# The opening of a two-layer encoder: the conditioning vector spread by its transfer, the vector table fetched first, low halves of the first weights on VectorE

## The chip, the cores and the metric

The kernel runs on one core of a Trainium2 chip. The metric is the device time of one execution in microseconds (us). Before the change it is 1388.13 us, the median of 3 runs (1387.73 to 1389.67). TensorE (PE) multiplies matrices, and its weight loads are shown as PEld; VectorE (DVE) and GpSimd (POOL) work elementwise on two tensors, ScalarE (ACT) on one; SyncE (SP) issues all the transfers of this kernel, in one queue.

## What is computed

The reference is an encoder of two layers over 512 tokens of width 1024. Each layer has a token mixer (layer 0 a gated short convolution, layer 1 a recurrent one) and an MLP. Each of these four parts is preceded by an RMS norm whose result is scaled and shifted by vectors that come from a conditioning vector `c`:

```
c_act = silu(c)
mod = c_act @ ada_w[i] + ada_b[i]          # six vectors of 1024 in each layer
sh1, sc1, gt1, sh2, sc2, gt2 = split(mod)
h = rmsnorm(x) * norm_g * (1 + sc1) + sh1
bch = h @ conv_w_in                        # layer 0: 1024 -> 3 x 1024
```

The change lies in these first lines of layer 0: `c_act`, the first two of its six vectors, the first norm, and the first part of `h @ conv_w_in`.

## The kernel before

Activations are kept transposed: 8 blocks of 128 features on the partitions by 512 tokens. To keep float32 accuracy every operand of a product is split in a high half (a rounded copy, made on ScalarE) and a low half (the original less the high one, a two-tensor subtraction), and a product is three passes: high by high, low by high, high by low.

The opening goes like this. SP issues `c` (one row of 1024 on one partition, L100), eight blocks of `x` (L102), the table `vec` of all small vectors (L103), and then for each of 8 blocks k two tiles of adaptation weights (`ada0`, 512 KB each, L374) and one tile of the first projection (`cin_a`, 128 x 896, L379). A transfer further down the queue waits until the eighth before it has landed, or until the buffer it fills is free.

ScalarE takes the sigmoid of `c`, VectorE multiplies it with `c` (L388), TensorE multiplies the row by a column of ones (L392) so that it stands on all 128 partitions, and ScalarE copies it from PSUM to `cb` (L397) between two squares. Meanwhile ScalarE squares the blocks of `x` (L226, L230) and VectorE adds them up (L231). TensorE sums over partitions (L402); square root (L406), reciprocal (L407) and four small products (L412, L413) spread the norm's factor. `keep_warm` matmuls (L365), whose result nobody reads, stand between.

Then comes a loop over the 8 blocks; I call it the block loop. For each k VectorE takes a dot of `cb` with an adaptation tile for the shift (L205, the first dot), makes the scale g0 (L420), the normed block t (L255), takes the dot for the scale of block k+1 (L205, the second dot), and makes the low half of h (L257). ScalarE makes the high half of h (L256) and the high half of the weights (L131), GpSimd their low half (L132). TensorE does 21 matmuls per block (L433: seven output tiles, three passes). After the loop the other 17 output tiles follow, one `linear` each of 24 matmuls (L171 to L173), on weights `wmain` (L136) whose low halves VectorE makes (L132).

TensorE, VectorE and ScalarE run the block loop in the order in which the code is written (the manual schedule). A scheduler orders what follows, and it may draw later instructions in between.

Of the kernel before, what the change touches and what calls it, by code (L numbers as in the profile page):

```python
# [10 lines left out]
F32 = mybir.dt.float32  # L11
F32R = mybir.dt.float32r
AF = mybir.ActivationFunctionType
ALU = mybir.AluOpType
# [3 lines left out]
P = 128  # L18
D = 1024
T = 512  # L20
# [34 lines left out]
def trunk(ctx: ExitStack, tc: tile.TileContext, x_in, vec_in, c_in, ada0, ada, cin_a, wmain,  # L55
          l1_in, g1_in, l2_in, g2_in, out, stop=None):
    nc = tc.nc
    V, A, G, PE = nc.vector, nc.scalar, nc.gpsimd, nc.tensor
# [9 lines left out]
    def uid():  # L68
        cnt[0] += 1
        return cnt[0]  # L70

    def bank(shape=(P, T)):
        return ps.tile(list(shape), F32, tag="ps", name=f"ps{uid()}")

    def sm(shape, bufs=2):
        return const.tile(list(shape), F32, tag="s" + "_".join(map(str, shape)), name=f"sm{uid()}", bufs=bufs)

    def big(shape=(P, 2, T), dt=F32R):
        return pool.tile(list(shape), dt, tag="b", name=f"b{uid()}", bufs=NBIG)
# [4 lines left out]
    def tmp(dt=F32):  # L84
        return pool.tile([P, T], dt, tag="t", name=f"t{uid()}", bufs=NTMP)

    def pair():
        t = big()
        return t[:, 0], t[:, 1]
# [6 lines left out]
    vec = const.tile([P, NVEC * KB], F32, name="vec")  # L96
    cb = big((P, D), F32)
    junk = big((P, D), F32)
    cr, cs = (big((P, D), F32)[0:1] for _ in range(2))
    nc.sync.dma_start(cr, c_in)  # L100
    for k in range(KB):
        nc.sync.dma_start(x[k], x_in[:, k * T:(k + 1) * T])  # L102
    nc.sync.dma_start(vec, vec_in)  # L103

    def vv(n, k=None):
        o = VEC[n] * KB
        return vec[:, o:o + KB] if k is None else vec[:, o + k:o + k + 1]
# [3 lines left out]
    ones = const.tile([P, P], F32, name="ones")  # L111
# [9 lines left out]
    def behind(ins, other):  # L121

        tc.add_manual_dep(ins.ins, other.ins.name, mybir.DependencyInfo(mybir.DependencyClass.NoSync,
                                                                        mybir.DependencyReason.DATA), reason="slots")
# [5 lines left out]
    def split(dst_hi, dst_lo, src, eng=None):  # L130
        A.copy(dst_hi, src)  # L131
        return (eng or V).tensor_tensor(dst_lo, src, dst_hi.bitcast(F32), op=ALU.subtract)  # L132
# [71 lines left out]
    def ada_dot(l, v, m, w):  # L204
        return V.tensor_tensor_reduce(junk, w, cb, 1.0, vv(f"ab{l}{v}", m), ALU.mult, ALU.add, mods[l, v][:, m:m + 1])  # L205
# [15 lines left out]
        ada_pump(max(0, want - ast["n"]))  # L221


    def add_sq(acc, k, sl):
        if k == 0:
            A.activation(acc[:, sl], x[k][:, sl], AF.Square)  # L226
        else:
            w = sl.stop - sl.start
            t = tmp()
            A.activation(t[:, :w], x[k][:, sl], AF.Square)  # L230
            V.tensor_tensor(acc[:, sl], acc[:, sl], t[:, :w], op=ALU.add)  # L231

    def new_acc():
        return tmp()
# [17 lines left out]
    def h_block(k, sl, pb, g, sh, hi, lo=None):  # L252
        w = sl.stop - sl.start
        t = tmp()
        V.scalar_tensor_tensor(t[:, :w], x[k][:, sl], g[:, k:k + 1], pb, op0=ALU.mult, op1=ALU.mult)  # L255
        A.activation(hi[:, sl], t[:, :w], AF.Identity, bias=sh[:, k:k + 1])  # L256
        return lambda: V.scalar_tensor_tensor(lo[:, sl], t[:, :w], sh[:, k:k + 1], hi[:, sl].bitcast(F32),  # L257
                                              op0=ALU.add, op1=ALU.subtract)
# [45 lines left out]
    def out_linear(acts, gt, nxt, side=lambda: None):  # L304

        n = NLAST
        for m in range(KB - n):
            pt = linear(1, acts)[0]
            residual(pt, m, FULL, gt)
            add_sq(nxt.acc, m, FULL)  # L310
            side()
        ws = w_take(n)

        def mm(pt, i, sl):
            for k in range(KB):
                passes(pt[:, sl], ws[i][0][:, k, :], ws[i][1][:, k, :], acts[k][0][:, sl], acts[k][1][:, sl],
                       k == 0, k == KB - 1)

        last_tiles(mm, gt, nxt)

    def last_tiles(mm, gt, nxt, spare=NFIRST):
        n = NLAST
        pt = [bank() for _ in range(n)]
        for sl in HALVES:
            for i in range(n):
                mm(pt[i], i, sl)
                if sl.start == 0 and i < spare:
                    w_conv(wst["pos"] + i + 1, True)
                residual(pt[i], KB - n + i, sl, gt)
                add_sq(nxt.acc, KB - n + i, sl)  # L330
                if sl.start:
                    for k in range(KB * i // n, KB * (i + 1) // n):
                        nxt.block(k, HALVES[0])
            if sl.start == 0:
                w_ahead()
                nxt.chain(sl)
# [26 lines left out]
    def keep_warm(n, after=None):  # L363
        for _ in range(n):
            m = PE.matmul(warm, ones, cmask, start=True, stop=True)  # L365
            if after is not None:
                behind(m, after)
# [3 lines left out]
    def ada_load(k):  # L371
        arw[k] = [big((P, D), F32) for _ in range(2)]
        for i in (1, 0):
            first = nc.sync.dma_start(arw[k][i], ada0[k, i])  # L374
        return first

    def weights(k):
        wr = big((P, NPRE * P), F32)
        nc.sync.dma_start(wr, cin_a[k])  # L379
        w = big((P, NPRE * P)), big((P, NPRE * P))  # L380
        split(*w, wr, G)
        return w

    g0 = const.tile([P, KB], F32, name="gs00")
    ada_load(0)
    with tc.manual_schedule(engines={mybir.EngineType.PE, mybir.EngineType.DVE, mybir.EngineType.Activation}):
        A.activation(cs, cr, AF.Sigmoid)
        V.tensor_tensor(cs, cr, cs, op=ALU.mult)  # L388
        keep_warm(NWARM)
        pcs = [bank() for _ in range(2)]  # L390
        for i in range(2):
            PE.matmul(pcs[i], ones[0:1], cs[:, i * T:(i + 1) * T], start=True, stop=True)  # L392
        acc = new_acc()
        for k in range(KB):
            add_sq(acc, k, FULL)
            if k in (5, 6):
                A.copy(cb[:, (k - 5) * T:(k - 4) * T], pcs[k - 5])  # L397
        keep_warm(2)
        A.activation(sm((P, 1)), epsn, AF.Sqrt)
        pm = bank((P, 4))  # L400
        for b in range(4):
            PE.matmul(pm[:, b:b + 1], acc[:, b * P:(b + 1) * P], ones[:, 0:1], start=True, stop=True)  # L402
        ada_dot(0, 1, 0, arw[0][1])
        keep_warm(1)
        sd = sm((P, 4))
        A.activation(sd, pm, AF.Sqrt, scale=1.0 / D, bias=epsn)  # L406
        V.reciprocal(sd, sd)  # L407
        pb = bank()
        dg = tmp()
        for b in range(4):  # L410
            c = slice(b * P, (b + 1) * P)
            V.tensor_scalar(dg[:, c], ident, sd[:, b:b + 1], None, op0=ALU.mult)  # L412
            PE.matmul(pb[:, c], ones, dg[:, c], start=True, stop=True)  # L413
        keep_warm(1)
        w = weights(0)
        h = []
        pts = [bank() for _ in range(NPRE)]
        for k in range(KB):
            ada_dot(0, 0, k, arw[k][0])
            V.scalar_tensor_tensor(g0[:, k:k + 1], mods[0, 1][:, k:k + 1], 1.0, vv("ng00", k), op0=ALU.add,  # L420
                                   op1=ALU.mult)
            h.append(pair())
            lo = h_block(k, FULL, pb, g0, mods[0, 0], *h[k])
            whi, wlo = w
            if k + 1 < KB:
                first = ada_load(k + 1)
                ada_dot(0, 1, k + 1, arw[k + 1][1])
            lo()
            if k + 1 < KB:
                w = weights(k + 1)  # L430
            for a, b in ((whi, 0), (wlo, 0), (whi, 1)):
                for i in range(NPRE):
                    PE.matmul(pts[i], a[:, i * P:(i + 1) * P], h[k][b], start=k == 0 and a is whi and not b,  # L433
                              stop=k == KB - 1 and b == 1)
# [5 lines left out]
    for j in range(KB):  # L440
        pc, pv, pg = [pts[3 * j + i] if 3 * j + i < NPRE else linear(1, h)[0] for i in range(3)]
        cs = tmp()
# [3 lines left out]
        t = tmp()  # L446
# [198 lines left out]
    with tc.manual_schedule(engines=MANUAL):  # L645
# [258 lines left out]
        t = 30  # L904
# [455 lines left out]
```

## Time and profile before

| | us |
|---|---|
| median of the runs | 1388.13 |
| the profiled execution | 1386.2 |
| its span, first to last instruction | 1384.2 |
| TensorE busy | 1309.3 (95%) |
| VectorE busy | 850.8 (61%) |
| ScalarE busy | 544.2 (39%) |
| GpSimd busy | 216.3 (16%) |

The mean granted clock of TensorE is 0.973 of full speed. TensorE carries 82% of the chain of work that ended last, VectorE 11%. In the first of 40 slices of the span (34.6 us each) TensorE is busy six tenths, in the second eight, and nine from the third on nearly everywhere.

### The profile page before, as it was taken

What the parts mean: (1) busy time and instruction counts of PE and PEld (TensorE: products, weight loads), DVE (VectorE), ACT (ScalarE), POOL (GpSimd) and SP (SyncE); (2) the same over time, 40 slices, a digit from 0 to 9 for tenths busy, and PEclk for the clock granted to TensorE, in tenths of its full rate; (3) what the DMA queues carried; (4) which work ended last, traced back from release to release, by engine and by line L of the source; (5) the groups of instructions that cost most, each with busy time, mean ns of one, the idle gap of its engine ahead of it and who ended that gap; (6) DMA issues with size and microseconds to landing.
All of it is one profiled execution on the core that took longest, in us unless ns stands there. A gap on an engine that the chain in (4) does not pass through costs nothing.

```text
span 1384.2 us, 20374 instructions
## 1 busy us (share of the span) xinstructions
PE 1309.3 (95%) x8182; PEld 1069.6 (77%) x8182; DVE 850.8 (61%) x1264; ACT 544.2 (39%) x924; POOL 216.3 (16%) x249
## 2 busy tenths in 40 slices
PE   6899999999999999899897599999989999999997
PEld 3688889888888888787576477777788888888886
DVE  6996668746747565736869835566574344343445
ACT  4233334323233234447552357765344133232331
POOL 2300020000000003523428512232300000000000
PEclk8999999999999999999999799999999999999998
DMA  8466432735646355301283413322222232222221
GB/s 326 148 241 244 184 122 107 262 127 202 231 147 250 136 197 190 119 16 61 73 236 110 107 52 124 102 84 67 72 77 76 91 107 92 94 104 91 98 101 61
DMA packets 83440, 184.44 MB, mean 133 GB/s; under 512 B 35377, under 2 KB 37681, under 8 KB 83346
## 3 DMA queue, kind: packets, MB, share of 16 engines
q1 hardware_dynamic: 83346, 183.14, 38.3%
q8 instruction: 64, 1.05, 0.3%
q14 instruction: 30, 0.25, 0.1%
HBM read 168.44 MB, written 13.63 MB: 132 GB/s over the span
## 4 chain that ended last, share of the span: by engine, by line
PE 82%; DVE 11%; ACT 3%; issue 2%; DMA 1%; POOL 1%; SPq 0%; DVEq 0%; ACTq 0%; POOLq 0%
PE ps L171 24%; PE ps L172 23%; PE ps L173 23%; DVE b L205 2%; DVE t L231 1%; DVE b L852 1%; DVE b L848 1%; PE ps L1002 1%; PE ps L1080 1%; PE ps L1047 1%; PE ps L1116 1%; PE ps L1099 1%; DVE w L132 1%; ACT w L131 1%; PE ps L630 1%
## 5 line engine op out<-in xcount | busy, mean ns | idle before, releaser
L173 PE MATMUL ps<-b,w 128*128 128x512 f32 (+1 forms) x1486 | 565.1, 380 | 10.5 <-DVE w L132 9.2
L171 PE MATMUL ps<-b,w 128*128 128x512 f32 (+1 forms) x1486 | 573.1, 386 | 1.1 <-DVE b L302 1.0
L172 PE MATMUL ps<-b,w 128*128 128x512 f32 (+1 forms) x1486 | 566.1, 381 | 5.1 <-POOL b L132 5.0
L131 ACT CAST w<-raw 128x1024 fp32r<-128x1024 f32 x176 | 185.0, 1052 | 486.0 <-PE ps L172 443.0
L173 PEld LDWEIGHTS ps<-b,w 128*128 128x128 f32 x1486 | 281.7, 190 | 64.4 <-DVE w L132 9.9
L172 PEld LDWEIGHTS ps<-b,w 128*128 128x128 f32 x1486 | 281.7, 190 | 57.5 <-POOL b L132 8.2
L171 PEld LDWEIGHTS ps<-b,w 128*128 128x128 f32 x1486 | 281.6, 190 | 56.4 <-issue 2.9
L132 DVE TENSOR_TENSOR w<-raw,w 128x1024 fp32r<-128x1024 f32 x172 | 210.7, 1226 | 145.6 <-ACT w L131 140.0
L302 DVE SCALAR_TENSOR_TENSOR b<-ps,mod,b 128x512 f32<-128x512 f32 (+1 forms) x116 | 80.3, 694 | 173.8 <-PE ps L173 173.5
L205 DVE CUSTOM_DVE_ANT_0 b<-b,b,vec 128x1024 f32<-128x1024 f32 x96 | 137.8, 1435 | 10.3 <-DMA b<-in_ada 9.8
L131 ACT CAST b<-t 128x512 fp32r<-128x512 f32 (+1 forms) x113 | 65.7, 590 | 98.2 <-DVE t L347 81.1
L132 DVE TENSOR_TENSOR b<-t,b 128x512 fp32r<-128x512 f32 x82 | 56.9, 699 | 28.8 <-ACT b L131 28.8
L529 POOL TENSOR_TENSOR b<-b,vec 128x512 f32<-128x512 f32 (+2 forms) x4 | 5.3, 1334 | 322.3 <-DMA b<-in_l 322.3
L256 ACT ACTIVATE b<-t,mod 128x256 fp32r<-128x256 f32 (+2 forms) x56 | 29.3, 536 | 58.1 <-DVE t L255 53.6
L171 PE MATMUL ps<-b,b 128*128 128x256 f32 (+1 forms) x152 | 47.6, 320 | 1.8 <-ACT b L256 1.7
L433 PE MATMUL ps<-b,b 128*128 128x512 f32 x168 | 41.7, 405 | 7.4 <-ACT b L256 7.4
L347 DVE TENSOR_TENSOR t<-t 128x512 f32<-128x512 f32 x64 | 43.5, 685 | 7.3 <-ACT t L346 7.3
L172 PE MATMUL ps<-b,b 128*128 128x256 f32 (+1 forms) x152 | 45.2, 298 | 1.7 <-POOL b L132 1.7
L231 DVE TENSOR_TENSOR t<-t,t 128x256 f32<-128x256 f32 (+1 forms) x47 | 41.4, 881 | 8.1 <-ACT t L230 7.5
L433 PEld LDWEIGHTS ps<-b,b 128*128 128x128 f32 x168 | 32.0, 194 | 17.4 <-ACT b L256 10.7
L132 POOL TENSOR_TENSOR b<-raw,b 128x1024 fp32r<-128x1024 f32 x9 | 22.1, 2459 | 148.7 <-ACT b L131 148.7
L173 PE MATMUL ps<-b,b 128*128 128x256 f32 (+1 forms) x152 | 45.0, 297 | 0.0
(205 smaller groups left out, 1345.6 us busy)
## 6 DMA issues: line engine op xcount, KB each, us to landing
raw<-in_wmain SPq DMA_DIRECT2D x185, 512.0 KB, 3.2
b<-in_ada SPq DMA_DIRECT2D x96, 512.0 KB, 5.7
sp<-b SPq DMA_DIRECT2D x8, 512.0 KB, 3.4
b<-sp SPq DMA_DIRECT2D x8, 512.0 KB, 4.8
b<-in_cin_a SPq DMA_DIRECT2D x8, 448.0 KB, 7.5
b<-in_x SPq DMA_DIRECT2D x8, 256.0 KB, 5.8
xs<-b SPq DMA_DIRECT2D x8, 256.0 KB, 2.2
sc<-t SPq DMA_DIRECT2D x8, 256.0 KB, 3.3
```

What stands on the lines that cost most here:

```text
L131: A.copy(dst_hi, src)
L132: return (eng or V).tensor_tensor(dst_lo, src, dst_hi.bitcast(F32), op=ALU.subtract)
L171: PE.matmul(dst, whi, ahi, start=start, stop=False)
L172: PE.matmul(dst, whi, alo, start=False, stop=False)
L173: return PE.matmul(dst, wlo, ahi, start=False, stop=stop)
L205: return V.tensor_tensor_reduce(junk, w, cb, 1.0, vv(f"ab{l}{v}", m), ALU.mult, ALU.add, mods[l, v][:, m:m + 1])
L231: V.tensor_tensor(acc[:, sl], acc[:, sl], t[:, :w], op=ALU.add)
L256: A.activation(hi[:, sl], t[:, :w], AF.Identity, bias=sh[:, k:k + 1])
L302: V.scalar_tensor_tensor(x[m][:, sl], pt[:, sl], gt[:, m:m + 1], x[m][:, sl], op0=ALU.mult, op1=ALU.add)
L347: V.tensor_tensor(r, r, r, op=ALU.mult)
L433: PE.matmul(pts[i], a[:, i * P:(i + 1) * P], h[k][b], start=k == 0 and a is whi and not b, stop=k == KB - 1 and b == 1)
L630: PE.matmul(pt[:, sl], w0, h[k][:, sl], start=start, stop=False)
```

## The change

`c` is read by a transfer that repeats its one row for each of 128 partitions; the sigmoid and the product then run on 128 x 1024 and write `cb` directly. The two matmuls with ones and the two copies from PSUM are gone. The table `vec` is issued in second place, ahead of `x`. Two `keep_warm` matmuls that stood after the eight squares are now written after the fourth and after the sixth square, two each. In the block loop the low half of the `cin_a` weights goes from GpSimd to VectorE: for k = 0 after t, for the others after the low half of h of the block before.

```diff
-    cr, cs = (big((P, D), F32)[0:1] for _ in range(2))
-    nc.sync.dma_start(cr, c_in)
+    cr, cs = (big((P, D), F32) for _ in range(2))
+    nc.sync.dma_start(cr, c_in.broadcast_to([P, D]))
+    nc.sync.dma_start(vec, vec_in)
     for k in range(KB):
         nc.sync.dma_start(x[k], x_in[:, k * T:(k + 1) * T])
-    nc.sync.dma_start(vec, vec_in)
...
         w = big((P, NPRE * P)), big((P, NPRE * P))
-        split(*w, wr, G)
-        return w
+        A.copy(w[0], wr)
+        return w, lambda: V.tensor_tensor(w[1], wr, w[0].bitcast(F32), op=ALU.subtract)
...
-        V.tensor_tensor(cs, cr, cs, op=ALU.mult)
+        V.tensor_tensor(cb, cr, cs, op=ALU.mult)
         keep_warm(NWARM)
-        pcs = [bank() for _ in range(2)]
-        for i in range(2):
-            PE.matmul(pcs[i], ones[0:1], cs[:, i * T:(i + 1) * T], start=True, stop=True)
         acc = new_acc()
         for k in range(KB):
             add_sq(acc, k, FULL)
-            if k in (5, 6):
-                A.copy(cb[:, (k - 5) * T:(k - 4) * T], pcs[k - 5])
-        keep_warm(2)
+            if k in (3, 5):
+                keep_warm(2, add[0])
...
             whi, wlo = w
+            if k == 0:
+                wlow()
             if k + 1 < KB:
                 first = ada_load(k + 1)
                 ada_dot(0, 1, k + 1, arw[k + 1][1])
             lo()
             if k + 1 < KB:
-                w = weights(k + 1)
+                w, wlow = weights(k + 1)
+                wlow()
```

The line numbers of the changed kernel are higher by 1 or 2, or lower by 2, near these places. Three places of the built programs matter below.

On TensorE the program begins with the `keep_warm` matmuls (they read cmask). Before, with what each waits for in brackets:

```order
L365 MATMUL ps_111<-cmask,ones 128x512 [waits Pool_49]
L365 MATMUL ps_111<-cmask,ones 128x512 x2
L392 MATMUL ps_124<-b_74,ones 128x512 [waits DVE_49]
L392 MATMUL ps_125<-b_74,ones 128x512
L365 MATMUL ps_111<-cmask,ones 128x512 x2
L402 MATMUL ps_157<-ones,t_128 128x1 [waits DVE_49]
L402 MATMUL ps_157<-ones,t_128 128x1 x3
```

In the changed kernel:

```order
L367 MATMUL ps_111<-cmask,ones 128x512 [waits Pool_49]
L367 MATMUL ps_111<-cmask,ones 128x512 x6
L400 MATMUL ps_153<-ones,t_124 128x1 [waits DVE_49]
L400 MATMUL ps_153<-ones,t_124 128x1 x3
L367 MATMUL ps_111<-cmask,ones 128x512
L411 MATMUL ps_163<-t_164,ones 128x128 [waits DVE_49] x4
```

The seven `keep_warm` matmuls stand in one row and wait for GpSimd's cmask alone: the place given to them by `add[0]` orders them, and adds no wait. The sum over partitions (L400, before L402) is next on TensorE.

On VectorE in the block loop, from the low half of h of block 0 to that of block 1, before (ISA is the dot and the read of its result):

```order
L257 SCALAR_TENSOR_TENSOR b_193<-t_194,mod_99,b_193 128x512
L205 ISA b_72,mod_99<-b_197,b_71,vec 128x1024
L205 ISA mod_99 128x1
L420 SCALAR_TENSOR_TENSOR gs_112<-mod_100,vec 128x1
L255 SCALAR_TENSOR_TENSOR t_233<-b_66,gs_112,ps_167 128x512
L205 ISA b_72,mod_100<-b_237,b_71,vec 128x1024
L205 ISA mod_100 128x1
L257 SCALAR_TENSOR_TENSOR b_232<-t_233,mod_99,b_232 128x512
```

In the changed kernel, from the subtraction for block 0:

```order
L384 TENSOR_TENSOR b_177<-b_174,b_176 128x896
L205 ISA b_72,mod_100<-b_194,b_71,vec 128x1024
L205 ISA mod_100 128x1
L259 SCALAR_TENSOR_TENSOR b_188<-t_189,mod_99,b_188 128x512
L384 TENSOR_TENSOR b_202<-b_199,b_201 128x896
L205 ISA b_72,mod_99<-b_193,b_71,vec 128x1024
L205 ISA mod_99 128x1
L418 SCALAR_TENSOR_TENSOR gs_112<-mod_100,vec 128x1
L257 SCALAR_TENSOR_TENSOR t_229<-b_66,gs_112,ps_163 128x512
L205 ISA b_72,mod_100<-b_233,b_71,vec 128x1024
L205 ISA mod_100 128x1
L259 SCALAR_TENSOR_TENSOR b_228<-t_229,mod_99,b_228 128x512
```

One subtraction (L384) has come into each block, and block 0 has two, its own and that of block 1.

On VectorE at the end of the block loop, from the first dot of block 7, before:

```order
L205 ISA b_72,mod_99<-b_431,b_71,vec 128x1024
L205 ISA mod_99 128x1
L420 SCALAR_TENSOR_TENSOR gs_112<-mod_100,vec 128x1
L255 SCALAR_TENSOR_TENSOR t_467<-b_69,gs_112,ps_167 128x512
L257 SCALAR_TENSOR_TENSOR b_466<-t_467,mod_99,b_466 128x512
L132 TENSOR_TENSOR w_496<-raw_493,w_495 128x1024
L132 TENSOR_TENSOR w_502<-raw_499,w_501 128x1024
```

In the changed kernel:

```order
L205 ISA b_72,mod_99<-b_427,b_71,vec 128x1024
L205 ISA mod_99 128x1
L418 SCALAR_TENSOR_TENSOR gs_112<-mod_100,vec 128x1
L132 TENSOR_TENSOR w_492<-raw_489,w_491 128x1024
L257 SCALAR_TENSOR_TENSOR t_463<-b_69,gs_112,ps_163 128x512
L132 TENSOR_TENSOR w_498<-raw_495,w_497 128x1024
L259 SCALAR_TENSOR_TENSOR b_462<-t_463,mod_99,b_462 128x512
L132 TENSOR_TENSOR w_576<-raw_501,w_575 128x1024
```

The scheduler has drawn the low half of the first `wmain` tile (w_492) ahead of the last t (t_463), and the second ahead of the last low half of h. The first matmul of the first `linear` (L171) likewise stands ahead of the last block's 21 matmuls on TensorE now.

## Rows read from the trace of the kernel before

**Rows 1.** Busy time in one stretch after the block loop.
```profile
core 0: us, PE busy (x) PEld busy (x) DVE busy (x) ACT busy (x) POOL busy (x), PEclk, DMA share, GB/s
72.00:130.00 58.00, 58.00 (x258) 48.04 (x257) 49.89 (x72) 21.17 (x28) 0.00 (x0) 1.00 0.64 240
```

**Rows 2.** Timeline of the opening: start, duration, instruction, count, idle before.
```profile
1.21 3.68 SPq L102 DMA_DIRECT2D b<-in_x  x8
2.26 4.92 PE L365 MATMUL ps<-cmask,ones 128*128 128x512 f32 x6 [2.26 <-POOL cmask L115]
...
11.40 0.19 DVE L480 TENSOR_SCALAR omu<-vec 128x48 f32<-128x48 f32 x1 [7.48 <-DMA vec<-in_vec]
...
17.13 0.63 ACT L230 ACTIVATE t<-b 128x512 f32<-128x512 f32 x1
...
17.79 0.69 DVE L231 TENSOR_TENSOR t<-t,t 128x512 f32<-128x512 f32 x1 [0.43 <-ACT t L230]
...
20.11 0.96 PE L402 MATMUL ps<-ones,t 128*128 128x1 f32 x8
...
22.29 2.14 POOL L132 TENSOR_TENSOR b<-b,b 128x896 fp32r<-128x896 f32 x1 [18.86 <-ACT b L131]
22.41 3.10 DVE L205 CUSTOM_DVE_ANT_0 b<-b,b,vec 128x1024 f32<-128x1024 f32 x1
...
25.44 0.15 DVE L420 SCALAR_TENSOR_TENSOR gs<-mod,vec 128x1 f32<-128x1 f32 x1
...
27.27 11.25 PE L433 MATMUL ps<-b,b 128*128 128x512 f32 x42 [3.28 <-ACT b L256]
```

**Rows 3.** Issues of the eight x blocks (L102).
```profile
DMA to landing us min/median/max: 3.0/5.8/6.4
```

**Rows 4.** Busy time, granted clock, DMA share and rate in three short stretches (columns of rows 1).
```profile
2.00:8.00 6.00, 4.92 (x6) 1.85 (x6) 0.97 (x5) 3.03 (x5) 1.30 (x8) 1.00 0.88 252
...
20.00:21.00 1.00, 1.00 (x10) 0.89 (x8) 0.00 (x0) 0.00 (x0) 0.00 (x0) 0.93 1.05 417
...
28.00:30.00 2.00, 2.00 (x7) 1.52 (x6) 2.00 (x2) 0.04 (x1) 1.88 (x1) 0.50 1.04 416
```

**Rows 5.** Timeline of the block loop, blocks 2 and 3.
```profile
37.93 1.28 DVE L205 CUSTOM_DVE_ANT_0 b<-b,b,vec 128x1024 f32<-128x1024 f32 x1
...
39.13 0.75 DVE L257 SCALAR_TENSOR_TENSOR b<-t,mod,b 128x512 fp32r<-128x512 f32 x1
39.68 2.18 POOL L132 TENSOR_TENSOR b<-b,b 128x896 fp32r<-128x896 f32 x1 [3.61 <-ACT b L131]
39.80 3.15 DVE L205 CUSTOM_DVE_ANT_0 b<-b,b,vec 128x1024 f32<-128x1024 f32 x1
...
42.88 0.15 DVE L420 SCALAR_TENSOR_TENSOR gs<-mod,vec 128x1 f32<-128x1 f32 x1
43.06 0.75 DVE L255 SCALAR_TENSOR_TENSOR t<-b,gs,ps 128x512 f32<-128x512 f32 x1
...
43.72 1.28 DVE L205 CUSTOM_DVE_ANT_0 b<-b,b,vec 128x1024 f32<-128x1024 f32 x1
43.84 0.72 ACT L256 ACTIVATE b<-t,mod 128x512 fp32r<-128x512 f32 x1 [4.24 <-DVE t L255]
44.47 0.92 ACT L131 CAST b<-b 128x896 fp32r<-128x896 f32 x1
44.62 5.07 PE L433 MATMUL ps<-b,b 128*128 128x512 f32 x21 [0.72 <-ACT b L256]
```

**Rows 6.** Timeline of block 7 and of the first matmuls after the loop.
```profile
66.30 0.75 DVE L255 SCALAR_TENSOR_TENSOR t<-b,gs,ps 128x512 f32<-128x512 f32 x1
...
67.91 5.10 PE L433 MATMUL ps<-b,b 128*128 128x512 f32 x21 [0.79 <-ACT b L256]
...
68.84 2.36 DVE L132 TENSOR_TENSOR w<-raw,w 128x1024 fp32r<-128x1024 f32 x2 [0.19 <-ACT w L131]
...
72.85 0.39 PE L171 MATMUL ps<-b,w 128*128 128x512 f32 x1
...
73.07 0.39 PE L172 MATMUL ps<-b,w 128*128 128x512 f32 x1
```

More of the change, by code (lines that the diff above doesn't have):

```diff
@@ L221, in ada_until @@
         ada_pump(max(0, want - ast["n"]))
+    add = [None]
     def add_sq(acc, k, sl):
@@ L230, in add_sq @@
             A.activation(t[:, :w], x[k][:, sl], AF.Square)
-            V.tensor_tensor(acc[:, sl], acc[:, sl], t[:, :w], op=ALU.add)
+            add[0] = V.tensor_tensor(acc[:, sl], acc[:, sl], t[:, :w], op=ALU.add)
     def new_acc():
@@ L414, in trunk @@
         keep_warm(1)
-        w = weights(0)
+        w, wlow = weights(0)
         h = []
```

## The prediction

> **What bounds the kernel now.** I read the table of busy time by stretch first, to see where TensorE has idle time that an edit could remove. From 72 to 130 us TensorE is busy 58.00 of 58.00 us [rows 1]: after the block loop it is the bound, and what comes before can only move its start. So the question is when the first matmul behind the block loop starts, and whether anything after it gives the time back. All edits lie ahead of that point.
>
> I then read the timeline of the opening. The useful work of TensorE starts at 27.27 us [rows 2]. The chain that leads there runs through VectorE and the keep_warm matmuls: VectorE has nothing to do for 7.48 us until the table has landed at 11.40; the product with `c` follows, the spread through TensorE, and the copies from PSUM stand between ScalarE's squares, so that the square of the last x block starts only at 17.13 and its addition at 17.79. The sum over partitions starts at 20.11, behind keep_warm matmuls. From there to 27.27 are 7.16 us, and 3.03 of them are one dot, from 22.41 to the scale at 25.44.
>
> Last I read the loop. A dot takes 1.28 us where GpSimd is quiet and 3.15 where it runs beside GpSimd's subtraction [rows 5]: the dot at 39.80 starts 0.12 us after the subtraction at 39.68, which ends at 41.86, and the next instruction follows at 42.88. Steps from start to start on VectorE: dot 1.20 (37.93 to 39.13), low half 0.67, the long dot 3.08, scale 0.18, t 0.66 (43.06 to 43.72). That is 5.79 per block, the time between the two dots at 37.93 and 43.72. TensorE needs less: 5.07 for a block's 21 matmuls with the tail of the last one, then 0.72 idle for ScalarE's high half. So VectorE sets the loop, and GpSimd's subtraction sets VectorE.
>
> **Terms, in the profiled execution's own time.**
>
> *The start.* The last x block is issued at about 4.5 us (eight issues over 3.68 from 1.21, [rows 2]) and lands 6.4 later at most [rows 3], at 10.9. Now 512 KB for `c` and 132 KB for the table (128 x 264 x 4 bytes) go ahead of it. The trace has no transfer that repeats a row. By the rate once the queue is full, 417 GB/s in [rows 4], `c` costs 1.3 us; by the rate of the x stretch, 252 GB/s, 2.1. I take 1.3, since its rows of 4 KB are as long as those of the adaptation tiles, and 0.5 for the table by the lower rate: the last x lands at 12.7. Square and addition take 1.35 (17.13 to 17.79 is 0.66, then 0.69): the sum is ready at 14.1. ScalarE and VectorE work on whole `c` tiles ahead of this, about 1.1 and 1.2 us; they run while x still arrives, and cost nothing unless `c` or the table lands after about 7 us.
>
> TensorE must be free then. Its seven keep_warm matmuls wait for nothing but cmask and run from 2.26. Three took 4.92 us [rows 2], two instructions each, which is 0.82 to 0.85 per instruction; fourteen end at 14.2 at the latest, earlier if the clock rises. So the sum over partitions starts at 14.1 instead of 20.11. The rest of the chain, 7.16, loses the stall of its dot, 3.03 less 1.20: 5.33. First real matmul at 19.43, 7.84 earlier. If `c` and the table cost nothing it would be 17.6; with 2.1 for `c` it is 20.2.
>
> *The block loop.* A GpSimd row beside it makes all eight first dots long; without one each loses 1.87 or so (3.08 less 1.20). Added is one subtraction of 128 x 896. No such row exists on VectorE. The subtraction of 128 x 1024 steps by 1.18 (two in 2.36, [rows 6]), the two-tensor operations on 512 columns by 0.67; on the line between them 896 cost 1.05. That is what I take; the ends are 0.67 and 1.18.
>
> By the Trainium skill ("VectorE: DVE Perf Modes", Mode 1x) such an operation yields one result per cycle at 0.96 GHz, which makes 0.93 for 896 columns; the row of 1024 columns is 0.11 above what it says for that size. By it the time would come out 1.0 us lower (eight times 0.12), inside the range below.
>
> The new period is 5.79 - 1.88 + 1.05 = 4.96. Does the subtraction wait? It needs ScalarE's high half of the weights. That cast starts 1.41 after t (44.47 against 43.06) and ends at 2.33; the subtraction comes after t, dot and low half, at 2.53. It doesn't wait, by 0.2. TensorE needs 21 x 0.227 = 4.77 per block (one matmul step is 0.22, 72.85 to 73.07 in [rows 6]; 5.07 less the tail of the last). VectorE still sets the loop, by 0.2 per block. Block 0 has two subtractions: 4.96 + 1.05 = 6.01 to the t of block 1, then six periods. At the end the low half of the first `wmain` tile now precedes the last t: 1.18 more. From the first t to the last: 6.01 + 6 x 4.96 + 1.18 = 36.95. Before it is 40.59: the first t starts 1.56 ahead of its matmul (43.06 to 44.62), at 25.71, the last at 66.30. Gain 3.64, with ends of 0.2 (1.18 instead of 1.05 in all eight is 1.0 lower; a missed cast up to 0.2 per block besides) and 5.1, where TensorE's 4.77 takes over.
>
> *After the loop.* One matmul of the first `linear` now runs in the gap ahead of block 7, for 0.22 less behind it. The transfer of the third `wmain` tile and two adaptation tiles now queue on SP behind VectorE's subtraction ahead of t; that third tile is wanted by TensorE two `linear`s of 24 matmuls later, 2 x 24 x 0.227 = 10.9 us after the loop, and its subtraction is done before the loop ends. TensorE has its work; I put nothing.
>
> Sum: 7.84 + 3.64 + 0.22 = 11.7. The profiled execution took 1386.2 (its span 1384.2 and 2.0 around it), so 1374.5; the median of the runs lies 1.9 above that execution, so **1376.4**.
>
> **Rivals.**
>
> *First blocks starved or cold.* The transfers gate the first blocks: with `c` at the lower rate everything shifts by 0.8, and if the tile of weights for block 1 lands late, VectorE now waits in line where GpSimd waited aside; half a microsecond to two. Beside it, TensorE's clock: block 0 runs at half rate before (0.50 in [rows 4]), after 3.28 us of idle time [rows 2]. With the stall gone that idle time is 1.4, so I expect full rate. If not, block 0 costs up to 4.8 more on TensorE, of which the 0.2 per block and the insertion at the end hide 2.6. Together 1378 to 1380.
>
> *The transfer of `c` is served one row after another* by one engine: the case that ends slower. A sixteenth of 417 GB/s is 26 GB/s, 512 KB in 20 us; of 252 GB/s, 33 us. Sigmoid stands ahead of every square on ScalarE, and the seventh x transfer waits in SP's queue for `c` to land. `c` landing at 22.5: sigmoid 1.05, eight squares of 0.63, one addition 0.7, sum at 29.3 instead of 14.1, 15.2 later: 1391.6; with 33 us 1405. It decides from where `c` lands after about 19. For it: no repeated row in the trace. Against it: destination and count of rows are those of an ordinary tile, and those are spread (rate above).
>
> The Trainium skill ("DMA: Bandwidth & Descriptors", Rules for kernel authors) states that a leading zero-stride repeat of c copies confines a transfer to at most c engines; with 128 copies that is no limit on 16, so by it `c` costs the 1.3 above. No run here shows it yet.
>
> *The stall of the dot is not GpSimd's.* Then the change adds 1.05 to a loop of 5.79. The matmuls start at 14.1 + 7.16 = 21.3, and the last t comes 7 x 6.84 + 1.05 + 1.18 = 50.1 after the first instead of 40.6: 9.5 later against 6.0 + 0.2 gained, 1391.4. Against it: all eight dots beside a GpSimd row are long and all others short, on the same tile shapes [rows 2, 5].
>
> *Given back later.* A wait behind the loop, where the scheduler's order of dots, casts and subtractions has changed up to some 60 us behind it, costs 1 to 5 us. TensorE's full stretch [rows 1] speaks against it. 1378 to 1381.
>
> **How the numbers follow.** Forecast 0.75, with a range of its own from 1374.5 to 1378.5. First blocks late or cold 0.13, given back later 0.06, `c` row by row 0.04, stall elsewhere 0.02. Ends of the start and loop terms that help together reach 1.8 + 1.5 below the forecast: 1373.2. Upward the range takes in the first and the last rival: 1381.5. A measurement of this kernel can tell about 0.2%, 2.8 us, from no change. Faster by more than that: 0.75 + 0.13 + most of 0.06, 0.92; slower: most of 0.06 for the two that end there, 0.05; the rest 0.03.
>
> **What would show it.** In the changed kernel's trace: GpSimd without rows between 3 and 70 us; the sum over partitions near 14 us, the first matmul of block 0 near 19.4; every dot of the loop 1.28; the new subtraction near 1.08 with a step of 1.05 and no wait ahead of it; blocks 4.96 apart; the first L172 near 61.4 instead of 73.07; TensorE full from there. The prediction is wrong in its start if ScalarE's sigmoid waits for `c` beyond 7 us or a keep_warm matmul ends after 14.2; in its loop if dots stay long or the subtraction waits for ScalarE or a transfer; and in its sum if TensorE shows idle time between 61 and 130 us.

## Result and the profile after

The changed kernel takes **1376.55 us** (median of 6 runs, 1375.38 to 1378.37), the kernel before 1389.83 beside it (6 runs, 1387.73 to 1392.14): ratio 0.9908, 95% interval 0.9895 to 0.992. The forecast was 1376.4, faster than before. The profiled execution took 1376.09, its span 1374.3, the mean granted clock 0.973 as before. First the timeline of the opening (start, duration, instruction, count, idle time before); it answers to [rows 2].

```profile
0.81 0.38 SPq L100 DMA_DIRECT2D b<-in_c  x1
...
2.27 7.95 PE L367 MATMUL ps<-cmask,ones 128*128 128x512 f32 x14 [2.27 <-POOL cmask L115]
...
4.91 1.06 ACT L389 ACTIVATE b<-b 128x1024 f32<-128x1024 f32 x1 [2.81 <-DMA b<-in_c]
5.43 0.19 DVE L481 TENSOR_SCALAR omu<-vec 128x48 f32<-128x48 f32 x1 [5.43 <-DMA vec<-in_vec]
...
6.94 1.22 DVE L390 TENSOR_TENSOR b<-b,b 128x1024 f32<-128x1024 f32 x1
7.19 4.66 ACT L232 ACTIVATE t<-b 128x512 f32<-128x512 f32 x7 [0.16 <-DMA b<-in_x]
8.08 5.46 DVE L233 TENSOR_TENSOR t<-t,t 128x512 f32<-128x512 f32 x7
...
13.60 1.87 PE L400 MATMUL ps<-ones,t 128*128 128x1 f32 x8 [3.38 <-DVE t L233]
...
16.80 1.28 DVE L205 CUSTOM_DVE_ANT_0 b<-b,b,vec 128x1024 f32<-128x1024 f32 x1
17.17 1.91 PE L411 MATMUL ps<-t,ones 128*128 128x128 f32 x8
...
19.12 0.75 DVE L257 SCALAR_TENSOR_TENSOR t<-b,gs,ps 128x512 f32<-128x512 f32 x1 [0.96 <-PE ps L411]
...
20.68 5.05 PE L434 MATMUL ps<-b,b 128*128 128x512 f32 x21 [0.56 <-ACT b L258]
```

`c` has landed 4.1 us after its issue (0.81 to 4.91), the table at 5.43 instead of 11.40. VectorE's seven additions then run without a break from 8.08: they set the end of the sum of squares, no longer the last x block. The sum over partitions starts at 13.60 (20.11 before), block 0 at 20.68 (27.27 before). But the two steps of TensorE between them take 1.87 and 1.91 us. The first took 0.96 before, and t waits 0.96 us for the second. The table by stretch (columns of rows 1) shows why:

```profile
2.00:8.00 6.00, 5.74 (x10) 2.56 (x11) 2.49 (x9) 2.53 (x5) 1.22 (x8) 1.00 0.97 310
10.00:20.00 10.00, 6.62 (x21) 4.56 (x20) 7.53 (x17) 4.45 (x8) 0.00 (x0) 0.66 1.03 412
20.00:30.00 10.00, 8.56 (x37) 6.68 (x37) 9.93 (x17) 3.02 (x4) 0.00 (x0) 1.00 1.02 407
...
62.00:130.00 68.00, 68.00 (x302) 56.31 (x301) 57.11 (x81) 23.09 (x30) 0.00 (x0) 1.00 0.64 234
```

The granted clock from 10 to 20 us is 0.66: TensorE stood idle for 3.38 us between the last keep_warm matmul, at 10.22, and the sum, and ran the chain largely at its lower level of 1.2 GHz. From block 0 on it has the full clock, and from 62 to 130 us it is busy throughout, as before in [rows 1].

The block loop, answering to [rows 5]:

```profile
30.66 1.28 DVE L205 CUSTOM_DVE_ANT_0 b<-b,b,vec 128x1024 f32<-128x1024 f32 x1
...
32.52 1.09 DVE L384 TENSOR_TENSOR b<-b,b 128x896 fp32r<-128x896 f32 x1
33.52 1.28 DVE L205 CUSTOM_DVE_ANT_0 b<-b,b,vec 128x1024 f32<-128x1024 f32 x1
...
34.92 0.75 DVE L257 SCALAR_TENSOR_TENSOR t<-b,gs,ps 128x512 f32<-128x512 f32 x1
...
35.59 1.28 DVE L205 CUSTOM_DVE_ANT_0 b<-b,b,vec 128x1024 f32<-128x1024 f32 x1
```

Both dots are 1.28 now, the subtraction steps by 1.00, and the two first dots are 4.93 apart instead of 5.79. The end of the loop answers to [rows 6]:

```profile
54.53 1.22 DVE L132 TENSOR_TENSOR w<-raw,w 128x1024 fp32r<-128x1024 f32 x1
55.66 0.74 DVE L257 SCALAR_TENSOR_TENSOR t<-b,gs,ps 128x512 f32<-128x512 f32 x1
...
56.55 0.47 PE L171 MATMUL ps<-b,w 128*128 128x512 f32 x1
57.21 5.05 PE L434 MATMUL ps<-b,b 128*128 128x512 f32 x21 [0.20 <-ACT b L258]
...
62.11 0.39 PE L172 MATMUL ps<-b,w 128*128 128x512 f32 x1
```

The first L172 starts at 62.11 instead of 73.07, 10.96 earlier: 6.59 from the start, 4.05 from the loop (first t to last t 36.54 instead of 40.59), 0.32 behind it. The same lines of the two traces are 10.8 to 10.9 apart from 566 to 674 us (in the time of the kernel before), 9.3 to 9.7 around 720 us and 9.3 at the last norm.

### The profile page after: what moved, and what is told of

It is laid out like the page before. It is cut to its first block, busy times and chain, and to the rows that moved or that the text cites. A ratio compares the mean times of both kernels' runs of the same rounds, so it can differ in the third digit from the quotient of the medians.

```text
span 1374.3 us, 20369 instructions
## 1 busy us (share of the span) xinstructions
PE 1308.5 (95%) x8182; PEld 1071.0 (78%) x8182; DVE 843.7 (61%) x1272; ACT 543.9 (40%) x922; POOL 197.5 (14%) x241
## 3 DMA queue, kind: packets, MB, share of 16 engines
q8 instruction: 64, 1.05, 0.3%
## 5 line engine op out<-in xcount | busy, mean ns | idle before, releaser
L173 PE MATMUL ps<-b,w 128*128 128x512 f32 (+1 forms) x1486 | 566.2, 381 | 10.7 <-DVE w L132 9.4
L171 PE MATMUL ps<-b,w 128*128 128x512 f32 (+1 forms) x1486 | 574.3, 387 | 1.4 <-DVE b L304 1.2
L172 PE MATMUL ps<-b,w 128*128 128x512 f32 (+1 forms) x1486 | 566.9, 381 | 4.3 <-POOL b L132 4.3
L173 PEld LDWEIGHTS ps<-b,w 128*128 128x128 f32 x1486 | 282.1, 190 | 64.7 <-DVE w L132 10.1
L172 PEld LDWEIGHTS ps<-b,w 128*128 128x128 f32 x1486 | 282.5, 190 | 57.1 <-POOL b L132 7.5
L171 PEld LDWEIGHTS ps<-b,w 128*128 128x128 f32 x1486 | 282.0, 190 | 57.5 <-issue 3.4
L205 DVE CUSTOM_DVE_ANT_0 b<-b,b,vec 128x1024 f32<-128x1024 f32 x96 | 122.9, 1281 | 9.7 <-DMA b<-in_ada 8.9
L171 PE MATMUL ps<-b,b 128*128 128x256 f32 (+1 forms) x152 | 46.9, 316 | 1.8 <-ACT b L258 1.7
L172 PE MATMUL ps<-b,b 128*128 128x256 f32 (+1 forms) x152 | 44.5, 294 | 1.8 <-POOL b L132 1.8
L173 PE MATMUL ps<-b,b 128*128 128x256 f32 (+1 forms) x152 | 44.3, 292 | 0.0
L1025 ACT COPY b<-ps 64x256 f32<-64x256 f32 x96 | 35.3, 367 | 15.5 <-PE ps L1018 11.7
```

Of the source, the lines that this page charges most:

```text
L171: PE.matmul(dst, whi, ahi, start=start, stop=False)
L172: PE.matmul(dst, whi, alo, start=False, stop=False)
L173: return PE.matmul(dst, wlo, ahi, start=False, stop=stop)
L1025: held(A.copy(dst[:, :, par], src) if (hh ^ par) in TA[n] else V.tensor_copy(dst[:, :, par], src))
```

## Experiments

My theory was this: the loop gained because GpSimd, reading SBUF, stalls VectorE's dot; the start gained because VectorE no longer waits for the table; the start fell short of its term because TensorE's clock was low in the chain. Rivals: the spread of `c` made the start; the dot's stall has another cause; the parts share one gain.

**One part alone: the low halves on VectorE.** The kernel before, with these lines alone:

```diff
-        split(*w, wr, G)
-        return w
+        A.copy(w[0], wr)
+        return w, lambda: V.tensor_tensor(w[1], wr, w[0].bitcast(F32), op=ALU.subtract)
...
+            if k == 0:
+                wlow()
...
-                w = weights(k + 1)
+                w, wlow = weights(k + 1)
+                wlow()
```

> Only the low halves of the first weights move to VectorE; c, the table and the keep_warm matmuls stay as before. If the two halves of the change are separate gains, the first dot of block 0 loses its stall (1.83 us), the loop's period falls from 5.79 to 4.93, and the first L172 comes at 66.9 us instead of 73.07: 6.2 us below the kernel before (ratio 0.9955). If the dots are long for another reason than GpSimd, they stay at 3.1 us, the period becomes 6.8, and the time is 1386 or more above the kernel before by 5 us (ratio 1.004).

Measured: 1383.35 us (1382.93 to 1383.92), ratio 0.9964, interval 0.9952 to 0.9975. The loop has its period of 4.93, t to t takes 36.53 as in the changed kernel, but the first L172 comes at 68.72, 1.8 later than expected, since the start gained nothing (timeline, then the granted clock by stretch):

```profile
20.37 1.71 PE L402 MATMUL ps<-ones,t 128*128 128x1 f32 x8
...
23.41 1.28 DVE L205 CUSTOM_DVE_ANT_0 b<-b,b,vec 128x1024 f32<-128x1024 f32 x1
23.78 1.91 PE L413 MATMUL ps<-t,ones 128*128 128x128 f32 x8
...
25.74 0.75 DVE L255 SCALAR_TENSOR_TENSOR t<-b,gs,ps 128x512 f32<-128x512 f32 x1 [0.97 <-PE ps L413]
```
```profile
20.00:30.00 10.00, 9.53 (x33) 6.65 (x32) 6.59 (x14) 2.64 (x4) 0.00 (x0) 0.69 1.03 409
```

The dot ahead of block 0 fell from 3.10 to 1.28, but t starts at 25.74, against 25.71 worked out for before: here TensorE's two steps ran at the low clock (1.71 and 1.91), and t waited for them. In this execution a stall removed on one engine was taken up by the next one in line.

**The other part alone: the opening.** The changed kernel with the low halves back on GpSimd:

```diff
-        A.copy(w[0], wr)
-        return w, lambda: V.tensor_tensor(w[1], wr, w[0].bitcast(F32), op=ALU.subtract)
+        split(*w, wr, G)
+        return w
...
```

> Only c's repeated transfer, the table in second place and the moved keep_warm matmuls; the low halves stay on GpSimd. If the halves are separate, the sum over partitions starts at 13.6 us as in the changed kernel, the first dot of block 0 is long again and block 0 starts at 21.6, the period is 5.79, the first L172 comes at 67.9: 5.2 us below the kernel before (ratio 0.9963). If the opening's gain is lost behind the slower loop, L172 comes at 72 to 73 and the ratio is 0.999 to 1.000.

Measured: 1381.88 us (1380.92 to 1386.05), ratio 0.9957, interval 0.9944 to 0.9969. The loop has its old period of 5.79, block 0 starts at 22.09, 0.5 later than expected, the first L172 at 67.88 as expected.

```profile
17.09 2.15 POOL L132 TENSOR_TENSOR b<-b,b 128x896 fp32r<-128x896 f32 x1 [13.76 <-ACT b L131]
17.22 3.10 DVE L205 CUSTOM_DVE_ANT_0 b<-b,b,vec 128x1024 f32<-128x1024 f32 x1
...
22.09 5.05 PE L431 MATMUL ps<-b,b 128*128 128x512 f32 x21 [1.32 <-ACT b L258]
```

The sum starts at 14.02, 0.4 later than in the changed kernel's first trace, and the chain from it to block 0 takes 8.07 instead of 7.08: the long dot beside GpSimd costs 1.0 there. The two parts alone make 0.9964 x 0.9957 = 0.9921.

**The changed kernel again,** beside these two on the same chip.

> The changed kernel once more, beside the others on the same chip. Theory: the first L172 again near 62.1 us, 11 us earlier than before; what lies between 11 and the difference of a single pair of runs (10 to 13) is the scatter of the second layer, which differs from execution to execution by about 1.5 us either way. Ratio 0.990 to 0.993. Rival: the time is lost again at a fixed place behind 670 us, and then the same place shows the same step of 1.2 us in this trace.

Measured: 1377.72 us (1374.39 to 1379.57), ratio 0.9921, interval 0.9907 to 0.9935.

```profile
13.85 1.05 PE L400 MATMUL ps<-ones,t 128*128 128x1 f32 x8 [2.51 <-DVE t L233]
```

By the medians the parts gain 5.2 and 6.7 us and the whole 10.8, so they add, to about 1 us. The first L172 came at 61.43. Block 0 started at 20.02, 6.17 after the sum, instead of 7.08: here the seven keep_warm matmuls ended later, at 11.34, TensorE stood idle for 2.51 us and not 3.38 ahead of the sum, and the clock fell later (0.83 from 10 to 20 us).

The sign named for the rival is there too. From the first L768 (L767 before) to the last L727 (L726 before), behind 660 us, this trace takes 35.1 us, the first trace of the changed kernel 35.3, the kernel before 33.8. But the two traces of the parts alone take 35.3 and 35.0 us for the same stretch, though they share no line of the change; that speaks for the one trace of the kernel before being the odd one. The part on why the prediction was right comes back to it.

**The table behind x again.**

```diff
-    nc.sync.dma_start(vec, vec_in)
     for k in range(KB):
         nc.sync.dma_start(x[k], x_in[:, k * T:(k + 1) * T])
+    nc.sync.dma_start(vec, vec_in)
```

> The changed kernel with the table of vectors issued behind the eight x blocks, as before. Theory (the table's place matters, because VectorE takes the two small operations on the table ahead of the product with c and of all additions): the table lands near 11.5 us instead of 5.4, the product with c starts near 12 instead of 6.94, seven additions of 0.7 to 0.78 follow from 13.2, the sum over partitions starts at 18 to 18.5 instead of 13.6, block 0 of the loop at 23.5 to 25 instead of 20.7, and the kernel takes 3 to 4.5 us longer than the changed one, 1380 to 1381. Rival (the 0.5 us of transfer is all that the place decides, VectorE catches up behind it): block 0 at 20 to 21, the same time as the changed kernel.

Measured: 1381.63 us (1378.12 to 1385.13), ratio 0.9941, interval 0.992 to 0.9963.

```profile
11.98 0.19 DVE L481 TENSOR_SCALAR omu<-vec 128x48 f32<-128x48 f32 x1 [8.06 <-DMA vec<-in_vec]
...
13.28 5.46 DVE L233 TENSOR_TENSOR t<-t,t 128x512 f32<-128x512 f32 x7
...
18.80 1.86 PE L400 MATMUL ps<-ones,t 128*128 128x1 f32 x8 [7.23 <-DVE t L233]
...
25.88 4.42 PE L434 MATMUL ps<-b,b 128*128 128x512 f32 x18
```

VectorE waits 8.06 us for 132 KB that only two small operations need, with the product and seven additions queued behind them. The sum starts 5.20 later than in the changed kernel, and block 0 too: 0.3 and 0.9 beyond the ends of the expectation. The chain between them took the 7.08 of the changed kernel's first trace, at the low clock here as well. Against the run of the next experiment, made beside it, it is 4.7 us slower by the medians; the intervals of the two ratios overlap slightly, so the claim rests on the traces.

**c spread by TensorE, the rest of the change in place.**

```diff
-    cr, cs = (big((P, D), F32) for _ in range(2))
-    nc.sync.dma_start(cr, c_in.broadcast_to([P, D]))
+    cr, cs = (big((P, D), F32)[0:1] for _ in range(2))
+    nc.sync.dma_start(cr, c_in)
...
+            if k in (5, 6):
+                A.copy(cb[:, (k - 5) * T:(k - 4) * T], pcs[k - 5])
+        keep_warm(2)
...
```

The two matmuls with ones are back too, and the two keep_warm matmuls stand where they stood before.

> The changed kernel, but c is fetched as one row and spread over the partitions by two matmuls with ones and two copies on ScalarE, as before; the table stays in second place and the low halves on VectorE. Theory (the start was gained by the table's place, the spread over partitions by the transfer is worth the two copies of ScalarE less what its 512 KB cost): x lands some 1 us earlier, the last square starts up to 1.3 later than without the copies, the sum over partitions at 14 to 15, block 0 within 1.2 us of the changed kernel's 20.7, the kernel 1376 to 1378. Rival (the spread by the transfer carries the start): the sum over partitions near 18 to 20 and block 0 near 25 to 27, 1381 to 1383.

Measured: 1376.95 us (1375.46 to 1378.02), ratio 0.9906, interval 0.9887 to 0.9925.

```profile
13.62 1.12 PE L402 MATMUL ps<-ones,t 128*128 128x1 f32 x8 [2.05 <-DVE t L231]
...
19.79 5.05 PE L436 MATMUL ps<-b,b 128*128 128x512 f32 x21 [0.74 <-ACT b L256]
```

The sum starts at 13.62, to 0.02 us where it starts in the first trace with `c` spread by its transfer, and the time is the same within the scatter. So of the start's edits the place of the table brought the gain; neither the spread nor the moved keep_warm matmuls changed the time by what can be measured.

**GpSimd busy with writes.** Each block gets useless work, read by nobody:

```diff
+        G.tensor_copy(spare[:, 0:1], w[0][:, 0:1].bitcast(F32))
+        for _ in range(5):
+            G.memset(spare, 0.0)
...
```

> The changed kernel with useless work for GpSimd in each block of the loop: a copy of one column of the high half, which orders it behind ScalarE's cast, then five memsets of 128x384 on a spare tile; its result is read by nobody. Theory (what stalls a VectorE dot is GpSimd reading SBUF beside it): dots stay 1.28, the subtraction 1.08, the period 4.93 to 5.0, the time 1374 to 1379. Rival (any busy GpSimd stalls VectorE's operation of two SBUF inputs): dots or subtractions beside the memsets grow by 1 us or more, the period to 6 or longer, 1384 or more.

Measured: 1376.39 us in one run, period 4.93.

```profile
42.38 1.09 DVE L387 TENSOR_TENSOR b<-b,b 128x896 fp32r<-128x896 f32 x1
42.39 1.13 POOL L384 COPY spare<-b 128x1 f32<-128x1 f32 x1 [2.42 <-ACT b L383]
...
43.38 1.28 DVE L205 CUSTOM_DVE_ANT_0 b<-b,b,vec 128x1024 f32<-128x1024 f32 x1
43.57 2.33 POOL L386 MEMSET spare<- 128x384 f32 x5
```

The memsets lie beside the dot and cost it nothing. The copy of one column, 0.19 us in three of the blocks, takes 1.13 here, where it starts 0.01 after VectorE's subtraction, and ends 0.05 after it (1.11 and 1.13 in the two blocks behind it): the stall goes in the other direction too.

**GpSimd busy with reads.**

```diff
+        for _ in range(2):
+            G.tensor_tensor(spare, wr[:, :384], w[0][:, :384].bitcast(F32), op=ALU.subtract)
...
```

> The changed kernel with useless work for GpSimd in each block of the loop: two subtractions of 128x384 from the two tiles of the block's weights into a spare tile; their result is read by nobody. Theory (GpSimd reading two SBUF tiles stalls VectorE's operations of two SBUF inputs): in each block one of the dots or the subtraction that overlaps is 1 to 1.9 us longer, the period 5.8 to 6.9, the time 1382 to 1391. Rival (the stall in the kernel before came from the tile shared between the two engines' chain, or from the size of 128x896): dots stay 1.28 and the period 4.93.

Measured: 1386.49 us in one run, period 6.50.

```profile
37.16 2.84 POOL L385 TENSOR_TENSOR spare<-b,b 128x384 f32<-128x384 f32 x2 [3.68 <-issue]
37.22 1.91 DVE L386 TENSOR_TENSOR b<-b,b 128x896 fp32r<-128x896 f32 x1
39.05 2.03 DVE L205 CUSTOM_DVE_ANT_0 b<-b,b,vec 128x1024 f32<-128x1024 f32 x1
...
41.86 1.28 DVE L205 CUSTOM_DVE_ANT_0 b<-b,b,vec 128x1024 f32<-128x1024 f32 x1
```

The two subtractions on GpSimd make VectorE's subtraction 0.82 longer and the dot behind it 0.75, two operations where one was expected: 1.57 per block, which is 6.50 less 4.93. The dot that runs beside no GpSimd row stays 1.28. Neither 128 x 896 nor a result that somebody waits for is needed for it, nor a shared tile: the dot reads `cb` and an adaptation tile, GpSimd the two tiles of weights. The Trainium skill ("SBUF — State Buffer", Who interferes with whom) says that a VectorE instruction with two SBUF inputs contends with a GpSimd instruction that reads SBUF, not with one that only writes; these two runs agree, by 1.57 and 0.00 us per block.

**More keep_warm matmuls,** ten in a row instead of seven:

```diff
-NWARM = 3
+NWARM = 6
```

> The changed kernel with ten keep_warm matmuls in a row ahead of the sum over partitions instead of seven; nothing else. Theory (what the start fell short of the forecast by is TensorE's low clock in the chain from the sum to block 0): granted clock near 1.00 from 10 to 20 us, the sum at 13.4 to 13.6 in 1.05 us instead of 1.87, block 0 at 18.8 to 18.9 instead of 20.7, the kernel 1.8 us shorter than the changed one run beside it. Rival (something else ends last ahead of t, such as the dot or a transfer): block 0 stays near 20.7 whatever the clock.

Measured: 1377.33 us (1374.07 to 1378.68), ratio 0.9908, interval 0.9885 to 0.9932.

```profile
13.98 1.04 PE L400 MATMUL ps<-ones,t 128*128 128x1 f32 x8
...
15.90 1.16 PE L411 MATMUL ps<-t,ones 128*128 128x128 f32 x8
...
19.38 0.97 PE L434 MATMUL ps<-b,b 128*128 128x512 f32 x3 [1.46 <-ACT b L258]
```
```profile
10.00:20.00 10.00, 8.54 (x33) 4.43 (x32) 9.16 (x18) 6.38 (x10) 0.00 (x0) 1.00 1.03 413
```

The full clock, the two steps in 1.04 and 1.16, and 5.40 from the sum to block 0: the forecast of that chain was 5.33. The sum itself came 0.4 later than expected, and block 0 at 19.38 is 0.5 late. The time is that of the changed kernel measured beside it:

> The changed kernel once more, as the measure for the two others of this call: 1375 to 1378, ratio 0.990 to 0.993; block 0 between 20.0 and 20.7, since its clock falls at a somewhat different time in each execution.

Measured: 1377.49 us (1377.17 to 1378.71), ratio 0.9916, interval 0.9897 to 0.9936.

```profile
13.47 1.05 PE L400 MATMUL ps<-ones,t 128*128 128x1 f32 x8 [1.97 <-DVE t L233]
```

Its chain took 5.61 (13.47 to 19.08), after 1.97 us of idle time: in this execution only 0.2 was left to gain, where the first profile of the same kernel had lost 1.7. Block 0 at 19.08 is even earlier than with ten matmuls, and below the 20.0 to 20.7 expected; the first L172 came at 60.51. The expected 1.8 was worked out from the one first profile. That the low clock lengthens the chain is shown, its mean cost is not.

**Ten keep_warm matmuls, and the low halves of the first two `wmain` tiles held behind the last low half of h:**

```diff
-NWARM = 3
+NWARM = 6
...
+            if wst["behind"] is not None:
+                behind(wst["last"], wst["lo"])
...
-            lo()
+            wst["lo"] = lo()
```

> The changed kernel with three more keep_warm matmuls at the start (ten in a row instead of seven), and the low halves of the first wmain tiles held behind the low half of h of block 7. If the chain from the sum over partitions to block 0 is long because TensorE runs it at the low clock, the clock stays at 1.00 from 6 us on, the sum takes 0.96 instead of 1.87, block 0 starts near 18.9 instead of 20.7; and the last t comes 1.2 earlier: TensorE's work behind the loop starts 2.9 us earlier (ratio 0.9885 to the kernel before). If VectorE sets that chain whatever the clock, block 0 stays at 20.7 and only 1.2 us are gained.

Measured: 1374.37 us (1373.47 to 1378.23), ratio 0.9907, interval 0.9892 to 0.9921.

```profile
18.84 5.06 PE L436 MATMUL ps<-b,b 128*128 128x512 f32 x21 [1.47 <-ACT b L260]
```
```profile
54.39 0.39 PE L173 MATMUL ps<-b,w 128*128 128x512 f32 x1
...
59.61 0.39 PE L175 MATMUL ps<-b,w 128*128 128x512 f32 x1
```

Block 0 comes at 18.84, and the first `linear` goes on behind the loop at 59.61 instead of 62.11, one matmul further on, since two of its matmuls now stand ahead of block 7 (L175 here is L173 of the changed kernel, which comes at 62.33: 2.7 earlier, of the 2.9 expected). Once more, beside the changed kernel:

> The kernel with ten keep_warm matmuls and with the low halves of the first two wmain tiles held behind the last low half of h, once more, beside the changed kernel on the same chip. By its trace the first linear begins 2.5 us earlier than in the changed kernel (59.61 against 62.11): 2.0 to 3.0 us shorter than the changed kernel, a ratio near 0.990 against 0.992. If the rest of the kernel gives it back: the same time within 1 us.

Measured: 1374.35 us (1373.67 to 1375.58), ratio 0.9894, interval 0.9873 to 0.9915. Both times it is some 3.2 us below the changed kernel by the medians (1374.37 and 1374.35 against 1377.72 and 1377.49), about 0.23%, and 1.9 and 3.1 us by the ratios. The intervals of the ratios overlap, so I call it probably better than the changed kernel, not shown. In the second pair of traces the same lines are 1.2 apart at 150 us and 2.6 to 2.7 from 552 us on. The difference of 1.4 between is in one place, a norm at 190 us (granted clock of the changed kernel measured beside it, then of this one):

```profile
185.00:200.00 15.00, 13.11 (x95) 12.72 (x94) 9.59 (x18) 6.24 (x11) 4.91 (x2) 0.89 0.32 107
```
```profile
185.00:200.00 15.00, 13.11 (x107) 12.69 (x106) 11.41 (x22) 7.24 (x14) 4.91 (x2) 1.00 0.28 97
```

TensorE stands idle for 1.89 us there in both. After it the clock fell in the one execution and not in the other. It did not fall in the first profile of the changed kernel either (1.00), and it did in the first profile of this one (0.77). So that part of the difference is no effect of the edit as far as the traces tell.

## Why the prediction was right

*The sum over partitions,* forecast for 14.1, started at 13.60, for another reason than the one given. `c` and the table cost less than the 1.8 put down: the last x block was issued at 5.4 and landed at most 5.8 later, by 11.2 instead of 12.7. VectorE's additions ended last, at 13.54. The prediction had put the work ahead of them at nothing unless `c` or the table landed after about 7; both had landed by 5.43, and VectorE set the end all the same. That the two misses nearly cancel is luck. The rival that `c` is served row by row needed it to land after about 19; it landed at 4.91. The trace agrees with the rule of the Trainium skill named there ("DMA: Bandwidth & Descriptors", Rules for kernel authors): a row repeated 128 times was not confined to one engine, for 512 KB landed in 4.1 us, where the prediction's estimate for one engine was 20.

*The chain from the sum to block 0* is the step that failed: 7.16 less the dot's stall, 5.33, measured 7.08. The stall did go (the dot is 1.28, in [rows 2] 3.10), but TensorE's two steps took its place: 1.87 for the sum against the 0.96 of [rows 2], and 1.91 for the steps ahead of t, which take 1.16 at the full clock (ten matmuls). I had allowed that the keep_warm matmuls end "earlier if the clock rises" and drew no consequence: they ended at 10.22 instead of 14.2, TensorE then stood idle for 3.38 us, and its clock fell. The prediction looked for a low clock in block 0 alone, after the 1.4 of idle time it expected there; block 0 had the full clock. Without the idle time the chain takes 5.40 to 5.43 (ten matmuls), so the working of the term holds at the full clock. The start gained 6.59 instead of 7.84 in the first profile; the two later ones took 6.17 and 5.61 for the chain.

*The loop* gained 4.05 instead of 3.64: the mechanism as forecast, the step of the new subtraction 1.00 instead of 1.05, so the period 4.93 instead of 4.96. The line drawn between the rows of 512 and 1024 columns was too high by 0.05. No wait stands ahead of the subtraction. The lower end of 0.2 given for this term does not follow from its parts: 3.64 less 1.0 and less eight times 0.2 is 1.0. GpSimd as the cause is shown from both sides: removed in the first experiment, brought back by reads alone in the one with 128 x 384. The 0.93 for 896 columns, an estimate from the Trainium skill ("VectorE: DVE Perf Modes", Mode 1x), was too low by 0.07.

*Behind the loop* 0.32 instead of 0.22. The first L172 came at 62.11, 0.7 later than forecast (61.43 and 60.51 in the later profiles); the profiled execution ended 1.6 above the forecast of 1374.5. The other 0.9 arose behind 660 us. That the median meets the forecast to 0.15 us is luck: it lies 0.5 above the profiled execution, where the prediction added 1.9, and that makes up for the 1.6. By the medians of the three comparisons the changed kernel was 13.3, 10.8 and 10.4 below the kernel before.

*Given back later* is not excluded. TensorE is full from 62 to 130 us, and 10.8 of 10.96 were still there at 674 us. Behind it all three traces of the changed kernel need 35.1 to 35.3 us for the stretch in which the kernel before needs 33.8. But there is only one trace of that kernel, of an execution (1386.2) that was 1.7 to 3.6 us faster than its medians (1387.89 to 1389.83), and the changed kernel with GpSimd's useless reads passed the same stretch in 32.4. Whether the change costs something there or that one trace was a lucky one stays open.

## What to carry to other kernels

A transfer of 132 KB issued last can hold up a whole engine if a small operation that needs it stands early in that engine's order: 4.7 us here by the medians and 5.2 in the traces, for a change of one line. Work given to GpSimd because it is idle is not free beside VectorE: ask which of its instructions read SBUF, and what of VectorE's lies beside them. And when a wait is removed, price every step that is left at the clock it will then run at, from the idle time that the new order leaves TensorE.

## What the runs showed of the hardware that was not expected

A GpSimd copy of a single column waits out a VectorE subtraction (1.13 us instead of 0.19), so the stall is mutual. A transfer that repeats one row of 4 KB for 128 partitions lands 4.1 us after its issue and hardly delays what is behind it: the stretch of 2 to 8 us moved 310 GB/s, against 252 before, and the last x block landed by 11.2 instead of 10.9 at the latest, behind `c` and the table.

And the same kernel does not always get the same clock. The chain of the opening took 7.08, 6.17 and 5.61 us in three profiles of it. The idle time ahead of it was not the same there, 3.38, 2.51 and 1.97 us: the keep_warm instructions, 0.85 us apart at first and 0.43 later, ended at 10.22, 11.34 and 11.50, since their pace changed at a different time. At the norm at 190 us, however, the idle time was 1.89 or 1.90 in all three, and the clock was 1.00, 1.00 and 0.89 over the next stretch. The chain alone differs by 1.5 us between executions; what decides when the clock changes stayed open.
